# Low halves of gate, branch and output-projection weights made by adding transfers

## The chip, the cores and the metric

The kernel runs on one core of a Trainium2 chip. The core has TensorE (PE in the profile), which multiplies matrices, VectorE (DVE), ScalarE (ACT) and GpSimd (POOL), which work on tiles, and SyncE (SP), which here only issues transfers. Each engine takes its instructions in the order in which they were written for it, and waits at an instruction until the semaphores it needs are set. Sixteen DMA engines do the transfers. Tiles lie in SBUF, 128 partitions wide; TensorE writes into eight PSUM banks of 128 x 512 float32.

The metric is the time of one execution on the device in microseconds. The kernel before takes 1569.97 us (median of three runs, 1569.14 to 1570.35).

## The reference

Two layers of a bidirectional encoder, with 512 tokens of 1024 channels in float32. One layer:

```
h = rms_norm(x);  proj = h @ w_in
c_q, c_kv, k_rope, gq, gk, gv, pool_in, gate_logits = split(proj)
o_mla  = mla_branch(c_q, c_kv, k_rope, ...)    # latent attention, 8 heads
o_gqa  = gqa_branch(gq, gk, gv, ...)           # 8 query heads, 2 key heads
o_pool = pool_branch(pool_in, ...)             # windows 2, 4, 8, 16
gates  = sigmoid(gate_logits)                  # 3 x 1024 per token
merged = gates[0] * (o_mla @ w_branch_mla) + gates[1] * (o_gqa @ w_branch_gqa)
       + gates[2] * (o_pool @ w_branch_pool)
x = x + merged @ w_out
u = depthwise_conv(rms_norm(x) @ ffn_w_up);  u_gate, u_val = split(u)
x = x + (silu(u_gate) * u_val) @ ffn_w_down
```

## The kernel before

**Two halves.** TensorE takes operands in a rounded float32 form (fp32r). To keep float32's accuracy, each operand is written as a rounded high half and the low half that the rounding left, and a product is three matmuls (`mm3`, which calls `mm`, line 522): high x high, high x low, low x high. For a weight the halves are `wh` and `wl`, for the normalised input `HH` and `HL`, for the merged branches `mgh` and `mgl`, for the branch outputs pairs such as `oph` and `opl`, for softmax numerators `ph` and `pl`.

**The stream of weights.** All weights come in one stream, in the order of use. SyncE's queue fetches stretches of up to 1024 columns into `raw` tiles, of which there are three; one holds two pieces of 512 columns. A piece of 512 columns is four 128 x 128 blocks, and for 512 tokens it feeds 4 x 3 matmuls. `_widths` lists the pieces of a layer up to the FFN, `_layer_units` adds those of the FFN and gives each a kind, and `_stream` deals them onto transfers. `w_split` makes the halves of the next piece. For kind "p", ScalarE copies the piece into `wh` (line 296, a helper's line that all of ScalarE's operations have), and VectorE or GpSimd subtracts it from the raw piece into `wl` (line 303, likewise a helper's); `pick` takes the engine by what the planner's clock holds free first, with a bias (`W_BIAS`, 2.54 us). For kind "u", which before only some pieces of the FFN have, `by_transfer` is used, as it also is for three of the seven forms in which the FFN's down weights come (there the tiles are named `fh` and `fl`):

```
A.activation(hi, r, AF.Copy)                      # high half, rounded
A.activation(lo, f(hi), AF.Copy, scale=-1.0)      # its negative
nc.gpsimd.dma_start(f(lo), r, accum_op=ALU.add)   # line 434: raw is added on
```

The transfer is issued from GpSimd's queue and adds the raw piece to the negated high half in SBUF. A raw tile is free for the next fetch when the low half of its last piece is done.

`wnext` hands out the next piece and has the pieces ahead of it split. How far ahead depends on the kinds that come:

```
kinds_ = [units[min(j + i, len(units) - 1)][0] for i in (0, LAP, LAF)]
n = LAF if any(k not in "pu" for k in kinds_) else LAP if "u" in kinds_[:2] else LA
```

with `LA, LAP, LAF = 3, 4, 6`. The pairs `wh`, `wl` have six buffers.

**What sets the order.** A planner in the kernel's Python keeps a clock (`Clock`) with a cost for each operation and a time at which each engine is free. Chains of steps on the other engines are written at the moment at which the clock says that their inputs are ready. So the order in which each engine gets its instructions follows from these costs, and a piece of another kind moves other instructions too: `copy` picks between ScalarE and VectorE by the same clock.

**The stages of a layer.** Input projection, with the pool branch; then the gates and branch products of the three branches (`gates`), 24 gate units of two pieces each and 12 branch units of two pieces. These are used as filler: `attention` goes through a plan of steps for eight heads (score matmuls `ps_S`, whose row maxima `nm` go by a small DMA into a row of the queries, `qb<-nm`; probabilities `ps_ST` or `ps_mi`, exponential on ScalarE, halves `ph` and `pl`; products with the values into `ps_AV`; a running sum `vt`, whose product with `unit` ends a head), and before each step that is not ready by the clock it writes filler units. GQA attention comes first, then the latent (MLA) attention, and what remains of the gates and branches fills in behind. There is one PSUM bank for scores (`S`), and two or one for each of the other tags. While GQA attention runs, the values (`vm`) and queries and keys (`MQ`, `MK`) of the MLA heads are made out of filler. Then comes the output projection, 8 tiles of two pieces each. As each tile ends, VectorE adds it to the residual `XM` and makes the scaled input `hn`, ScalarE the high half `HH` and the squares `sqt`, VectorE `HL`, and GpSimd sums the squares into `sq`; for the FFN's down weights' way of multiplying, sums of tiles (`tt`, `tf`) are made too. The FFN's first up-projection piece follows the output projection without a pause in TensorE's order.

Of the kernel before, what the change touches and what calls it, by code (L numbers as in the profile page):

```python
# [19 lines left out]
T = 512  # L20
D = 1024
KC = D // P
# [52 lines left out]
def _order(br):  # L75

    r, lag = [], LAG[br]
    for m in range(KC + lag):  # L80
        r += [(k, pos.index(m)) for k, b, pos in EXTRA if b == br and m in pos]
        if m < KC:
            r.append(("g", m))
        if m >= lag:
            r.append(("b", m - lag))
    return r


WIDTHS = {"g": [T, T], "b": [T], "q": [384, 384], "n": [256], "v": [256]}
# [3 lines left out]
def _widths():  # L93

    r = [384] * KC + [T] * 8 + [T] * KC + [288] * MID + [T] + [288] * (KC - MID)
    for br in (2, 1, 0):
        late = []
        for k, _ in _order(br):
            if k in "nv":
                late = WIDTHS[k]  # L100
            else:
                r += WIDTHS[k][:1] + late + WIDTHS[k][1:]
                late = []
    return r + [T] * (2 * KC)


def _groups():
# [4 lines left out]
def _ffn():  # L112

    toks, late = [], []
    for g, (c0, c1) in enumerate(_groups()):
        dealt = len(late) - (KEEP * SIZES[g - 1] if g == len(SIZES) - 1 else 0)
        for n, c in enumerate(range(c0, c1)):
            if g == 0:  # L120
                toks += [("u", c, 0), ("u", c, 1)]
                continue
            now = late[:dealt * (n + 1) // (c1 - c0) - dealt * n // (c1 - c0)]
            late = late[len(now):]
            for f in FORMS:
                toks.append(("f", c, f))
                if f in SPOTS:
                    k = SPOTS.index(f)
                    toks += now[len(now) * k // len(SPOTS):len(now) * (k + 1) // len(SPOTS)]
        late += [("d", g, m, i) for m in range(KC) for i in range(c1 - c0)]  # L130
    return toks + late


def _layer_units():

    r = [("p", wd) for wd in _widths()]
    for tok in _ffn():
        if tok[0] == "u":
            r += [("u", T), ("p", T), ("next",)]
        elif tok[0] == "f":  # L140
            r.append(tok)
        elif (tok[2] * SIZES[tok[1]] + tok[3]) % 4 == 0:
            r.append(("u" if tok[1] < len(SIZES) - 1 else "p", T))
    return r


def _stream():
# [4 lines left out]
    for kind, *u in _layer_units() * L:  # L152
        if kind == "next":
            plain = (plain + 1) % (2 * SIZES[0])
            if plain and plain >= 2 * SIZES[0] - 8:
                early.append(len(slots))
                slots.append(T)
                alone.append(True)
            continue
        if kind == "f":  # L160
            if u[1] == FORMS[0]:
                first, fresh = len(pieces), True
                for _ in range(4):
                    if early:
                        pieces.append((early.pop(0), 0, T))
                        continue
                    pieces.append((len(slots), 0, T))
                    slots.append(T)
                    alone.append(True)
            units.append((u[1], first))  # L170
            continue
        if len(slots) <= KC or fresh or alone[-1] or slots[-1] + u[0] > 1024:
            slots.append(0)
            alone.append(False)
        fresh = False
        pieces.append((len(slots) - 1, slots[-1], u[0]))
        slots[-1] += u[0]
        units.append((kind, len(pieces) - 1))
# [1840 lines left out]
```

## Time and profile before

| | |
|---|---|
| median of the runs | 1569.97 us (1569.14 to 1570.35) |
| profiled execution, its own time | 1569.55 us |
| its span in the profile | 1567.7 us |
| TensorE busy | 1546.2 us (99%) |
| VectorE busy | 1171.7 us (75%) |
| ScalarE busy | 1012.9 us (65%) |
| GpSimd busy | 809.8 us (52%) |
| hardware transfer queue q1 | 32.9% of the sixteen DMA engines' span |
| software transfer queue q0 | 19.3% of it |
| granted TensorE clock | 1.00 |

The profile is of one execution. Its span leaves out 1.85 us that lie around it (1569.55 - 1567.7). In rows of instructions stand the line, the engine, the operation, the tile written and those read (buffer numbers left out), the shape, the count, then busy time and mean in ns, then idle time ahead and what ended it. A row of the timeline begins with start and duration in us. Waits are put down to the releaser that came last.

### The profile page before, as it was taken

The numbers are of one execution on the slowest core, as the hardware profiler recorded it, in microseconds if no ns is written. First come the engines' busy times: TensorE is split into PE (matmuls) and PEld (weight loads), VectorE is DVE, ScalarE is ACT, GpSimd is POOL, SyncE is SP. The second block draws the span as 40 slices with busy tenths as digits, with TensorE's granted clock in tenths as the row PEclk, the third lists the DMA queues.
The fourth block names the chain that finished last, engine by engine and source line by source line (L and its number), as shares of the span: only waits on it lengthen the run. The fifth ranks groups of instructions, "written<-read, shape, count | busy, mean of one in ns | idle before, by whom it ended". The sixth has DMA issues, their size and how long they took to land.

```text
span 1567.7 us, 24155 instructions
## 1 busy us (share of the span) xinstructions
PE 1546.2 (99%) x8265; PEld 1339.0 (85%) x8265; DVE 1171.7 (75%) x1932; ACT 1012.9 (65%) x1908; POOL 809.8 (52%) x822
## 2 busy tenths in 40 slices
PE   9999989999999999999999999899999999999999
PEld 8888878888878999999898888788887789999997
DVE  6867886875777888877756688768757778888785
ACT  5557766763457878777544577666635577777763
POOL 3984867764653222222488658768546533222222
PEclk9999999999999999999999999999999999999999
DMA  5432224313378877886434322343243688787863
GB/s 201 126 115 80 75 74 145 118 66 124 108 181 199 194 179 174 193 195 145 130 120 133 114 74 70 93 135 115 59 143 108 176 200 201 166 192 174 211 119 101
DMA packets 124684, 216.61 MB, mean 138 GB/s; under 512 B 29328, under 2 KB 51344, under 8 KB 124560
## 3 DMA queue, kind: packets, MB, share of 16 engines
q1 hardware_dynamic: 91152, 162.93, 32.9%
q0 software_dynamic: 28512, 51.92, 19.3%
q8 instruction: 65, 1.06, 0.3%
q10 hardware_dynamic: 4896, 0.21, 0.2%
q14 instruction: 59, 0.48, 0.1%
HBM read 149.41 MB, written 13.63 MB: 104 GB/s over the span
## 4 chain that ended last, share of the span: by engine, by line
PE 84%; DVE 7%; issue 3%; ACT 3%; POOL 2%; DMA 1%; SPq 0%; ACTq 0%; POOLq 0%; DVEq 0%
PE ps_acc L522 35%; PE ps_AV L522 16%; PE ps_ST L522 14%; PE ps_S L522 10%; PE ps_mi L522 10%; DVE XM L303 1%; DVE tt L303 1%; POOL wl L303 1%; DMA wl<-raw 1%; DVE mgl L303 1%; ACT mgh L296 1%; DVE sq L303 0%; DVE gt L307 0%; ACT wh L296 0%; DVE XM L307 0%
## 5 line engine op out<-in xcount | busy, mean ns | idle before, releaser
L303 POOL TENSOR_TENSOR wl<-raw,wh 128x512 fp32r<-128x512 f32 (+3 forms) x261 | 335.6, 1292 | 273.3 <-ACT wh L296 252.7
L296 ACT ACTIVATE wh<-raw 128x512 fp32r<-128x512 f32 (+2 forms) x453 | 265.4, 605 | 49.9 <-DVE raw L303 10.5
L434 POOL DMA_DIRECT2D wl<-raw x96 | 83.7, 872 | 246.8 <-ACT sx L296 160.4
L434 POOL DMA_DIRECT2D fl<-raw x102 | 89.2, 874 | 154.2 <-ACT fl L296 69.2
L522 PE MATMUL ps_acc<-HH,wl 128*128 128x512 f32 x416 | 163.2, 392 | 4.4 <-DMA wl<-raw 4.4
L522 PE MATMUL ps_acc<-HH,wh 128*128 128x512 f32 x416 | 163.4, 393 | 3.9 <-DVE vm L303 2.9
L522 PE MATMUL ps_acc<-HL,wh 128*128 128x512 f32 x416 | 162.8, 391 | 0.4 <-DVE HL L303 0.4
L307 DVE SCALAR_TENSOR_TENSOR a<-u,prm,a 128x511 f32<-128x511 f32 x176 | 133.7, 761 | 34.9 <-ACT a L296 34.1
L311 DVE TENSOR_REDUCE nm<-ps_S 128x1 fp32r<-128x512 f32 x128 | 87.7, 685 | 36.1 <-PE ps_S L522 34.7
L296 ACT ACTIVATE a<-u,prm 128x512 f32<-128x512 f32 x88 | 71.2, 811 | 63.2 <-DVE u L303 63.2
L522 PE MATMUL ps_acc<-tf,wh 128*128 128x256 f32 x544 | 100.1, 282 | 0.0
L522 PEld LDWEIGHTS ps_acc<-HH,wl 128*128 128x128 f32 x416 | 78.1, 188 | 23.1 <-DMA wl<-raw 6.2
L522 PEld LDWEIGHTS ps_acc<-HH,wh 128*128 128x128 f32 x416 | 78.3, 188 | 20.7 <-issue 4.4
L522 PEld LDWEIGHTS ps_acc<-tf,wh 128*128 128x128 f32 x544 | 88.5, 189 | 6.2
L522 PEld LDWEIGHTS ps_acc<-HL,wh 128*128 128x128 f32 x416 | 78.2, 188 | 17.1 <-DVE HL L303 1.1
L303 DVE TENSOR_TENSOR wl<-raw,wh 128x512 fp32r<-128x512 f32 (+2 forms) x97 | 71.7, 740 | 25.5 <-ACT wh L296 25.3
L522 PE MATMUL ps_AV<-HH,wh 128*128 128x256 f32 (+1 forms) x248 | 82.1, 331 | 0.0
L522 PE MATMUL ps_AV<-HH,wl 128*128 128x256 f32 (+1 forms) x248 | 82.0, 331 | 0.0
L522 PE MATMUL ps_AV<-HL,wh 128*128 128x256 f32 (+1 forms) x248 | 82.0, 331 | 0.0
L522 PE MATMUL ps_acc<-tf,wl 128*128 128x256 f32 x272 | 76.6, 282 | 0.0
L296 ACT ACTIVATE ps_ST<-ps_ST 128x512 f32<-128x512 f32 x86 | 49.8, 581 | 33.1 <-PE ps_ST L522 31.7
L296 ACT ACTIVATE fl<-fh 128x512 fp32r<-128x512 f32 x102 | 64.5, 633 | 3.2
(428 smaller groups left out, 4969.7 us busy)
## 6 DMA issues: line engine op xcount, KB each, us to landing
raw<-w SPq DMA_DIRECT2D x160, 512.0 KB, 3.7
raw<-w SPq DMA_DIRECT2D x140, 256.0 KB, 4.3
fl<-raw POOLq DMA_DIRECT2D x102, 256.0 KB, 5.4
wl<-raw POOLq DMA_DIRECT2D x96, 256.0 KB, 4.6
raw<-w SPq DMA_DIRECT2D x14, 384.0 KB, 3.0
XM<-x SPq DMA_DIRECT2D x16, 256.0 KB, 3.1
dtq<-tr SPq DMA_DIRECT2D x16, 192.0 KB, 1.9
dtk<-tr SPq DMA_DIRECT2D x16, 192.0 KB, 2.0
```

The costliest lines, as they stand in the source:

```text
L296: return self.eng.activation(out, in_, func, **k)
L303: return self.eng.tensor_tensor(out, *a)
L307: return self.eng.scalar_tensor_tensor(out, *a)
L311: return self.eng.tensor_reduce(out, in_, *a, **k)
L434: nc.gpsimd.dma_start(f(lo), r, accum_op=ALU.add)
L522: PE.matmul(o, lhsT=lhsT, rhs=rhs, start=start, stop=stop, skip_group_check=again)
```

## The change

The gate and branch pieces of all three branches and the pieces of the output projection get the kind "u"; for that `_widths` returns pairs of kind and width. These are 48 + 24 + 16 = 88 pieces in each layer. The input projection, the latent attention's own weights (kinds q, n, v of the order) and the FFN keep what they had.

```
 def _widths():
 
     r = [384] * KC + [T] * 8 + [T] * KC + [288] * MID + [T] + [288] * (KC - MID)
+    r = [("p", wd) for wd in r]
     for br in (2, 1, 0):
         late = []
         for k, _ in _order(br):
+            ws = [("u" if k in "gb" else "p", wd) for wd in WIDTHS[k]]
             if k in "nv":
-                late = WIDTHS[k]
+                late = ws
             else:
-                r += WIDTHS[k][:1] + late + WIDTHS[k][1:]
+                r += ws[:1] + late + ws[1:]
                 late = []
-    return r + [T] * (2 * KC)
+    return r + [("u", T)] * (2 * KC)
...
 def _layer_units():
 
-    r = [("p", wd) for wd in _widths()]
+    r = _widths()
```

Since `wnext` looks ahead by `LAP` where such pieces come, their halves are asked for four pieces ahead where it was three. The order of the engines moves as follows; the lines of the changed kernel are two further down.

TensorE at the end of layer 0's GQA attention. Before, the last piece of filler (`wh69`, `wl69`, out of which rows of the gate are left for later) stands ahead of the last head's probabilities:

```order
L522 MATMUL ps_acc_364_2375<-HH_81,wh69_2312 128x512
L522 MATMUL ps_acc_364_2375<-HL_82,wh69_2312 128x512
L522 MATMUL ps_acc_364_2375<-HH_81,wl69_2313 128x512
L522 MATMUL ps_ST_386_2479<-qa_323_2107,ka_80_594 128x512
L522 MATMUL ps_ST_386_2479<-qb_324_2108,kb_81_595 128x512
L522 MATMUL ps_AV_378_2433<-ph_376_2431,vg_76_590 128x512
```

After, the same piece stands ahead of the head before, and the four score matmuls of the last head (`ps_S`) come behind it:

```order
L524 MATMUL ps_acc_344_2339<-HL_82,wh69_2263 128x512
L524 MATMUL ps_acc_344_2339<-HH_81,wl69_2264 128x512
L524 MATMUL ps_ST_363_2446<-qa_324_2207,ka_80_594 128x512
L524 MATMUL ps_ST_363_2446<-qb_325_2208,kb_81_595 128x512
L524 MATMUL ps_S_367_2452<-ka_80_594,qa_326_2209 128x512
L524 MATMUL ps_AV_354_2386<-ph_352_2384,vg_76_590 128x512
L524 MATMUL ps_AV_354_2386<-pl_334_2253,vg_74_588 128x512
L524 MATMUL ps_S_368_2462<-ka_80_594,qa_326_2209 128x512
```

The next filler follows 24 attention matmuls later before, 45 after; in both, it starts at row 1010 of TensorE's order.

GpSimd at the end of the output projection in layer 0 (`wl129` is the first piece of the FFN). Before:

```order
L303 TENSOR_TENSOR wl127_4537<-raw67_4422,wh127_4536 128x512
L303 TENSOR_TENSOR sq_711_4267<-sq_711_4267,sqt_730_4498 128x512
L303 TENSOR_TENSOR wl128_4561<-raw67_4422,wh128_4560 128x512
L434 DMA wl129_4565<-raw68_4485 128x512
L303 TENSOR_TENSOR sq_711_4267<-sq_711_4267,sqt_740_4558 128x512
```

After:

```order
L436 DMA wl127_4591<-raw67_4530 128x512
L436 DMA wl128_4624<-raw67_4530 128x512
L305 TENSOR_TENSOR sq_711_4347<-sq_711_4347,sqt_730_4588 128x512
L436 DMA wl129_4652<-raw68_4581 128x512
L305 TENSOR_TENSOR wl130_4678<-raw68_4581,wh130_4677 128x512
```

The subtractions of `wl127` and `wl128` have become issues of transfers, and the sum of squares stands right ahead of `wl129`'s transfer.

GpSimd at the first gate pieces of layer 0 (`raw_863` holds the first two). Before:

```order
L303 TENSOR_TENSOR gqr_804<-gqr_804,rp_115_909 128x512
L303 TENSOR_TENSOR wl_963<-raw_863,wh_962 128x512
L303 TENSOR_TENSOR yt_806<-y_102_805,ssr_347 128x32
L303 TENSOR_TENSOR yt_806<-yt_806,y_102_805 128x32
L315 TENSOR_SCALAR yt_806<-yt_806 128x32
L303 TENSOR_TENSOR y_102_805<-yt_806,y_102_805 128x32
L303 TENSOR_TENSOR wl_988<-raw_863,wh_987 128x512
```

After:

```order
L436 DMA wl_930<-raw_863 128x512
L305 TENSOR_TENSOR gqr_804<-gqr_804,rp_115_909 128x512
L436 DMA wl_967<-raw_863 128x512
L305 TENSOR_TENSOR yt_806<-y_102_805,ssr_347 128x32
L305 TENSOR_TENSOR yt_806<-yt_806,y_102_805 128x32
```

The first transfer stands ahead of the rotary sum `gqr`, the second ahead of the small steps (`yt`, `y`) that make a reciprocal root, where before the subtractions came behind each.

Counted over the program, GpSimd's order has 176 transfers more and 166 subtractions fewer, VectorE's 10 subtractions fewer and some copies out of PSUM more (`MK` 0 to 6, `MQ` 2 to 10, `vm` 6 to 12, `ph` 46 to 52), and ScalarE's 176 negated copies more and those other copies fewer. TensorE has the same matmuls.

## The prediction

> **What bounds the kernel now.** I read the page first (busy times, costliest groups, DMA issues), then TensorE's waits, then windows of 20 us, then the timeline where a window falls short.
>
> ```profile
> span 1567.7 us, 24155 instructions
> PE 1546.2 (99%) x8265; PEld 1339.0 (85%) x8265; DVE 1171.7 (75%) x1932; ACT 1012.9 (65%) x1908; POOL 809.8 (52%) x822
> ```
>
> TensorE (PE) is the bound: 1546.2 of 1567.7 us, so that all its idle time is 21.5 us. The change leaves every matmul as it is; it can win only out of these 21.5 us, and lose by adding to them. The rate that a filled stage keeps:
>
> ```profile
> 351.65 18.38 PE ps_acc L522 x81
> ```
>
> 18.38/81 = 0.227 us for a matmul of 512 columns. Where the idle time lies:
>
> ```profile
> PE ps_acc L522 <- DMA wl<-raw: 4.4, 4, 2.3
> PE ps_acc L522 <- DVE vm L303: 2.9, 2, 1.4
> PE ps_ST L522 <- ACT vt L296: 2.5, 2, 1.3
> PE ps_AV L522 <- DVE ph L319: 1.7, 2, 0.9
> ```
>
> (Columns: tile waited in, releaser, us in all, times, longest.) There are two kinds. The first row is the entry into the FFN, where TensorE meets the first low half made by an adding transfer. The other three come twice each, once in a layer: the end of grouped-query (GQA) attention, where no gate or branch matmuls are left to fill in. Windows of the two places, with one filled stage between (span, then busy time and count of PE, PEld, DVE, ACT, POOL, clock, DMA share, GB/s):
>
> ```profile
> 140.00:160.00 20.00, 20.00 (x96) 16.93 (x95) 16.91 (x32) 16.88 (x32) 8.90 (x18) 1.00 0.25 73
> 200.00:220.00 20.00, 17.29 (x79) 13.90 (x78) 16.44 (x32) 14.03 (x29) 15.41 (x19) 1.00 0.23 79
> 980.00:1000.00 20.00, 16.60 (x72) 12.85 (x70) 17.66 (x33) 14.51 (x29) 14.52 (x18) 1.00 0.19 60
> 420.00:440.00 20.00, 18.59 (x81) 14.75 (x79) 17.73 (x25) 11.78 (x24) 14.14 (x12) 1.00 0.53 145
> 1200.00:1220.00 20.00, 17.48 (x75) 13.63 (x74) 17.62 (x26) 13.20 (x27) 12.79 (x11) 1.00 0.65 172
> ```
>
> **The change part by part.** In both layers 48 gate, 24 branch and 16 output-projection pieces, 176 in all, get their low half by copy, negated copy and adding transfer. The order of the changed kernel has 166 subtractions fewer on GpSimd (POOL), 10 fewer on VectorE (DVE), 176 negated copies more on ScalarE (ACT) and 176 transfers more in POOL's queue. The prices:
>
> ```profile
> L303 POOL TENSOR_TENSOR wl<-raw,wh 128x512 fp32r<-128x512 f32 x227 | 302.1, 1337 | 247.3 <-ACT wh L296 232.3 <-PE ps_acc L522 7.9 <-issue 2.9
> L303 DVE TENSOR_TENSOR wl<-raw,wh 128x512 fp32r<-128x512 f32 x83 | 61.5, 741 | 19.3 <-ACT wh L296 19.2
> L296 ACT ACTIVATE wl<-wh 128x512 fp32r<-128x512 f32 x96 | 60.7, 633 | 3.0
> L434 POOL DMA_DIRECT2D wl<-raw x96 | 83.7, 872 | 246.8 <-ACT sx L296 160.4
> wl<-raw POOLq DMA_DIRECT2D x96, 256.0 KB, 4.6
> q0 software_dynamic: 28512, 51.92, 19.3%
> ```
>
> Engine time: POOL 176 x 0.872 - 166 x 1.337 = -68 us; DVE -10 x 0.741 = -7 us, less some 20 copies out of PSUM that come over from ACT; ACT 176 x 0.633 = +111 us, less those copies. None of it is on PE's path by itself. The software queue took 19.3% of the span for 51.92 MB, 198 transfers of 256 KB, that is 0.193 x 1567.7/198 = 1.53 us of all sixteen engines each; 176 more are +269 us, some 17 points of share. In the gate stages (0.25) that is covered.
>
> Latency of one low half from the end of its high half: before 1.34 us; after 0.63 + 4.6 = 5.2 us, so 3.9 us later. The lookahead grows from 3 to 4 pieces where these pieces come, and one piece of four token blocks by three terms is 12 matmuls, 12 x 0.227 = 2.7 us. So a low half comes 1.2 us nearer to its use in a stage of PE work alone, and less where attention matmuls stand between. The slack in most of the attention stage is several us, which covers this. It is thin at the first gates:
>
> ```profile
> 97.12 1.48 POOL L303 TENSOR_TENSOR wl<-raw,wh 128x512 fp32r<-128x512 f32 x1
> 99.28 0.40 PE L522 MATMUL ps_acc<-HH,wl 128*128 128x512 f32 x1
> ```
>
> Made at 98.60, used at 99.28: slack 0.7 us, 1.2 later makes 0.5 us of stall, in each layer: **+1.0** (0 if the earlier high half is early enough; up to 3 if POOL, whose queue also holds the pool branch's and norm's work here, issues late).
>
> **Entry of the FFN.** Timeline of layer 0, and the releaser in layer 1:
>
> ```profile
> 422.36 0.48 DVE L315 TENSOR_SCALAR hn<-XM,prm 128x512 f32<-128x512 f32 x1
> 425.87 1.50 POOL L303 TENSOR_TENSOR sq<-sq,sqt 128x512 f32<-128x512 f32 x1
> 426.24 0.63 ACT L296 ACTIVATE wl<-wh 128x512 fp32r<-128x512 f32 x1
> 427.32 1.48 POOL L303 TENSOR_TENSOR wl<-raw,wh 128x512 fp32r<-128x512 f32 x1
> 427.57 1.51 DVE L315 TENSOR_SCALAR hn<-XM,prm 128x512 f32<-128x512 f32 x1
> 428.75 1.05 POOL L434 DMA_DIRECT2D wl<-raw  x1
> 434.98 0.50 PE L522 MATMUL ps_acc<-HH,wl 128*128 128x512 f32 x1 [1.00 <-DMA wl<-raw]
> ```
>
> ```profile
> 1206.59 0.92 POOL L434 DMA_DIRECT2D wl<-raw  x1
> 1214.13 0.50 PE L522 MATMUL ps_acc<-HH,wl 128*128 128x512 f32 x1 [2.29 <-DMA wl<-raw]
> ```
>
> The negated copy of the first FFN piece was done at 426.87, but its transfer was issued only at 428.75, behind the norm's sum and the last subtraction. Without that subtraction it goes at about 427.4, 1.3 us sooner; the wait of 1.00 goes, and of 2.29 about 1.3. The same row shows the other gain: the tensor_scalar that makes hn took 1.51 us beside POOL's subtraction, and 0.48 five microseconds earlier, and the reason that I see is POOL's subtraction of two SBUF inputs; so VectorE's chain to the next HH should quicken too. I take 1.0 + 1.3 + 0.2 = **-2.5**. The ends: -6, if all losses of both windows (1.4 + 2.5 us of PE's 20 in each) go and some 2 more at the later FFN pieces and the merge; +1, if the transfers now crowd one another. For that end, the landing times of this stage, from 425 to 480 us and from 1198 to 1212 us:
>
> ```profile
> DMA to landing us min/median/max: 3.3/5.9/6.8
> ```
>
> ```profile
> DMA to landing us min/median/max: 4.4/6.0/7.5
> ```
>
> In the output projection a piece is wanted every 2.7 us, and its transfer takes 1.53 us of the DMA engines: 0.56 of share on the raw loads. If that pushes landings past 7.5 us, the gain of layer 1 is lost.
>
> **End of GQA attention.** Here the change moves instructions. Before, 24 attention matmuls stand behind the last gate fill (215.31 to 224.55 us); after, 45, the scores of the last head among them.
>
> ```profile
> 202.88 0.40 PE L522 MATMUL ps_S<-ka,qa 128*128 128x512 f32 x1
> 203.38 1.58 DVE L303 TENSOR_TENSOR wl<-raw,wh 128x512 fp32r<-128x512 f32 x1
> 206.56 0.47 PE L522 MATMUL ps_acc<-HH,wh 128*128 128x512 f32 x1 [1.44 <-DVE vm L303]
> 211.71 0.68 DVE L311 TENSOR_REDUCE nm<-ps_S 128x1 fp32r<-128x512 f32 x1
> 212.46 0.48 ACTq L1385 DMA_DIRECT2D qb<-nm  x1
> 215.31 0.39 PE L522 MATMUL ps_ST<-qa,ka 128*128 128x512 f32 x1
> 224.55 0.39 PE L522 MATMUL ps_acc<-HH,wh 128*128 128x512 f32 x1
> ```
>
> ```profile
> qb<-nm ACTq DMA_DIRECT2D x16, 2.0 KB, 1.9
> ```
>
> ```profile
> L303 DVE TENSOR_TENSOR pl<-ps_ST,ph 128x512 fp32r<-128x512 f32 x86 | 58.5, 683 | 10.4 <-ACT ph L296 9.3
> ```
>
> Before, the last head's first score matmul ran at 202.88 and attention ended at 224.55: 21.67 us for 70 matmuls' worth of work (73, six of half width), 15.9 us, so 5.8 us lost. After, I lay the chain out by hand. The four score matmuls stand within ten rows and share one PSUM bank, so each waits for the row maximum of the one ahead: 0.39 + 0.68 and an estimated 0.2 of handoffs is 1.27 us, four times 5.1, and a pl of 0.68 stands in VectorE's order ahead of the last maximum: 5.8 us. The maxima then go by DMA, 1.9 us to landing, with another 0.3 of handoffs until the head's first probability matmul: 8.0 us for 19 matmuls, 4.3 us of work. Then come the same 24 matmuls as before, 9.24 us for 5.5 of work. Lost: 3.7 + 3.8 = 7.5 us, and VectorE comes about 1 us later to that point than before (eleven of its steps, some 0.7 us each, stand from the first maximum to where it was at 215.31 before: 7.7 us without any idle of its own), so 8.5 against 5.8: **+2.7 in each layer, +5.4**. Ends: 0, if the wait for vm of 1.44 goes with the subtraction at 203.38 and VectorE, which POOL delays less, has the scores ready sooner; +4.5 in each layer, +9, if ScalarE, 16.88 of 20 us busy at 140 us and given three or four copies more of 0.63 there, falls a further head behind.
>
> **The sum.** +5.4 + 1.0 - 2.5 = +3.9 on the profiled execution, 1569.55 us with 1.85 around the span; the runs' median is 1569.97. On that: 1573.9. What a measurement can tell from no change is about 0.2%, 3.1 us.
>
> **A rule against it.** The Trainium skill, "SBUF — State Buffer", section on the two separate sides, says that a transfer issued from GpSimd's queue cannot have its descriptors written while VectorE holds the shared port pair in a 2-port mode, and advises hardware queues. Here the issue beside hn took 1.05 us against a mean of 0.872, so the trace agrees in direction, with 0.2 us. By the rule each transfer would wait up to one such step of VectorE (0.48 us), and the sum would rise by at most that at the two thin places, some 1 us in all. My sum leaves it out.
>
> **The rivals.**
> 1. *The FFN entry wins more than the tail loses* (other side: faster). Mechanism: POOL's subtractions no longer stretch VectorE's two-input steps, in the output projection and at the end of GQA attention. For it: 1.51 against 0.48 above, and 1.58 for a DVE subtraction whose mean is 0.741. Against it: at the tail nearly all DVE steps read PSUM and take their 0.68 regardless. It decides where the tail costs under 1 us in each layer: -6 + 1 + 1 = -4, 1566.
> 2. *Terms cancel.* The tail at +1.3 in each layer (the wait for vm goes), first gates +0.5, entry -3.5: -0.4, 1569.6.
> 3. *Transfers land late.* If the share at 420 us (0.53) and 0.56 more saturate the DMA engines, raw tiles are held until the transfer is done, loads start later, and PE waits for wl through the output projection: 1 us for perhaps four of sixteen pieces, in each layer, on top of the sum without its gain: +6.4 + 8 = +14, 1584. Against it: one piece's 0.5 MB half-load and transfer fit 2.7 us, by 1.53 and the load's part.
> 4. *The order does not matter*, as the fill that is spent early is work that VectorE uses to catch up: part of 2.
>
> **Numbers.** Forecast (1572.5 to 1581): 0.46. Rival 1: 0.29. Rival 2 with 4: 0.20. Rival 3: 0.05. Slower by over 0.2% takes most of the forecast and rival 3 (0.49), within 0.2% the rest of the forecast and nearly all of rival 2 (0.22), faster rival 1 (0.29). The likeliest is 1573.9; its own range is 1572 to 1580. The range that leaves out no more than 2 in 10 goes from 1563.5 (near rival 1's full -6 with no tail loss) to 1581.
>
> **What would show it.** Tail: waits of PE in a window of some 25 us up to the end of GQA attention, now for DVE nm or a row DMA, 8 us and more; right if the layer loses 2 us or more there over before, wrong if under 1. First gates: a PE wait for DMA wl<-raw near 85 to 100 us. Entry: the wait for wl at 434 us gone, that at 1214 halved, hn at 0.5 to 0.6 us. ACT +111 us busy at most, POOL about 740, DMA share of the software queue near 36%. The forecast falls if the tail's loss stays at 5.8 us, or if PE waits for wl all along the output projection.

## The result and the profile after

The changed kernel takes 1577.41 us (median of four, 1575.26 to 1578.93) against 1569.56 (median of four): 1.005 times the time before, 95% interval 1.0037 to 1.0063. It is slower, as forecast; the forecast was 1573.9. The profiled execution took 1575.26 us with a span of 1573.4, 5.7 more than before.

The page of the changed kernel: span, busy times, the software queue and the groups that grew.

```profile
span 1573.4 us, 24580 instructions
PE 1550.5 (99%) x8265; PEld 1340.9 (85%) x8265; DVE 1146.9 (73%) x1940; ACT 1113.5 (71%) x2066; POOL 744.3 (47%) x832
q0 software_dynamic: 53856, 98.07, 36.3%
L436 POOL DMA_DIRECT2D wl<-raw x272 | 244.7, 907 | 508.6 <-ACT wl L298 235.5
L298 ACT ACTIVATE wl<-wh 128x512 fp32r<-128x512 f32 x272 | 172.0, 633 | 8.6
...
wl<-raw POOLq DMA_DIRECT2D x272, 256.0 KB, 4.5
```

The work moved as counted: POOL fell by 65.5 us to 744.3, ACT rose by 100.6, the software queue's share went from 19.3% to 36.3%. TensorE did the same matmuls and was busy 4.3 us longer, of which the clock, below, has a part. What TensorE waits for has turned round:

```profile
PE ps_S L524 <- DVE nm L313: 5.2, 10, 1.0
PE ps_ST L524 <- DMA qb<-nm: 3.1, 4, 1.2
PE ps_acc L524 <- DVE MQ L321: 2.0, 2, 1.0
PE ps_acc L524 <- DVE XM L309: 1.7, 2, 1.0
PE ps_ST L524 <- DVE vt L309: 1.5, 2, 0.7
```

The wait for low halves at the FFN's entry, 4.4 us, is gone from the list. In its place stand waits for row maxima and for their small transfers, and two for copies of MLA queries out of PSUM (`MQ`), which before were ScalarE's. Windows of 20 us over the places of the prediction, in its columns:

```profile
80.00:100.00 20.00, 19.09 (x96) 15.89 (x95) 12.33 (x23) 14.59 (x33) 18.54 (x29) 1.00 0.85 191
100.00:120.00 20.00, 19.01 (x87) 15.68 (x86) 10.69 (x22) 11.62 (x21) 6.62 (x9) 1.00 0.81 178
220.00:240.00 20.00, 18.02 (x70) 12.98 (x70) 16.23 (x32) 16.83 (x33) 7.65 (x10) 0.91 0.32 70
420.00:440.00 20.00, 20.00 (x90) 16.56 (x89) 15.84 (x25) 13.46 (x27) 9.60 (x10) 1.00 0.87 223
1200.00:1220.00 20.00, 20.00 (x90) 16.58 (x89) 16.37 (x26) 12.36 (x25) 9.95 (x10) 1.00 0.93 240
```

The end of the output projection is now full, 20.00 of 20 in both layers where it was 18.59 and 17.48, though the DMA share there is 0.87 and 0.93. (The same point of the program comes 4.0 and 6.6 us later now; windows moved by that, 424 to 444 and 1206.6 to 1226.6 us, have TensorE at 20.00 and 19.67.) The first gates, 20.00 in both windows before, are not. The end of GQA attention lies some 7 us later than before and shows fewer matmuls, and a mean clock of 0.91. Its timeline in layer 0, with the head before last's row of maxima ahead:

```profile
208.54 0.48 ACTq L1387 DMA_DIRECT2D qb<-nm  x1
213.90 0.51 PE L524 MATMUL ps_ST<-qb,kb 65*128 65x512 f32 x1 [1.23 <-DMA qb<-nm]
214.25 0.40 PE L524 MATMUL ps_S<-ka,qa 128*128 128x512 f32 x1
215.43 0.62 PE L524 MATMUL ps_S<-ka,qa 128*128 128x512 f32 x1 [0.32 <-DVE nm L313]
217.04 0.62 PE L524 MATMUL ps_S<-ka,qa 128*128 128x512 f32 x1 [0.53 <-DVE nm L313]
218.44 0.62 PE L524 MATMUL ps_S<-ka,qa 128*128 128x512 f32 x1 [0.32 <-DVE nm L313]
219.82 0.48 ACTq L1387 DMA_DIRECT2D qb<-nm  x1
221.73 0.50 PE L524 MATMUL ps_ST<-qb,kb 65*128 65x512 f32 x1 [0.34 <-DMA qb<-nm]
...
228.55 0.63 PE L524 MATMUL ps_AV<-ph,vg 128*128 128x512 f32 x1
228.97 0.63 PE L524 MATMUL ps_AV<-pl,vg 128*128 128x512 f32 x1
231.44 0.39 PE L524 MATMUL ps_acc<-HH,wh 128*128 128x512 f32 x1
```

The four scores start 1.40 us apart on average ((218.44 - 214.25)/3), the row leaves 5.57 us after the first score, and attention ends 17.2 us after it. That is the chain of the prediction. New are the transfer issued at 208.54, which landed only at some 213.8 (its counterpart in layer 1 also took 5.3 us), and, in this layer alone, matmuls at the very end that start 0.42 us apart.

To compare kernels I add up what each matmul starts later than TensorE's rate allows after the one ahead, stage by stage, from the starts in the trace (losses under 0.08 us left out). Both layers together, in us; "gates" reaches from the end of the input projection to the third head of attention, "attention" from there through GQA and MLA attention, "entry" over merge, output projection and the FFN's first pieces.

| kernel | gates | attention | entry | span |
|---|---|---|---|---|
| before | 1.0 | 13.9 | 9.4 | 1567.7 |
| changed | 6.1 | 23.9 | 1.8 | 1573.4 |

So the change lost 5.1 + 10.0 us and won 7.6. That is 7.5 in these stages, while the span rose by 5.7; outside them the same count has about 1 us less than before (4.9 and 3.8), and what falls under 0.08 us is not counted. Of the 10.0, the ends of GQA attention have 3.5 and 3.3 (5.4 to 8.9 and 5.5 to 8.7), and the rest lies earlier in attention.

### The profile page after: what moved, and what is told of

It is laid out like the page before. It is cut to its first block, busy times and chain, and to the rows that moved or that the text cites. A ratio compares the mean times of both kernels' runs of the same rounds, so it can differ in the third digit from the quotient of the medians.

```text
span 1573.4 us, 24580 instructions
## 1 busy us (share of the span) xinstructions
PE 1550.5 (99%) x8265; PEld 1340.9 (85%) x8265; DVE 1146.9 (73%) x1940; ACT 1113.5 (71%) x2066; POOL 744.3 (47%) x832
## 3 DMA queue, kind: packets, MB, share of 16 engines
q0 software_dynamic: 53856, 98.07, 36.3%
## 5 line engine op out<-in xcount | busy, mean ns | idle before, releaser
L436 POOL DMA_DIRECT2D wl<-raw x272 | 244.7, 907 | 508.6 <-ACT wl L298 235.5
L298 ACT ACTIVATE wl<-wh 128x512 fp32r<-128x512 f32 x272 | 172.0, 633 | 8.6
L305 POOL TENSOR_TENSOR wl<-raw,wh 128x512 fp32r<-128x512 f32 (+3 forms) x95 | 116.9, 1239 | 94.3 <-ACT wh L298 92.1
L524 PEld LDWEIGHTS ps_acc<-HH,wl 128*128 128x128 f32 x416 | 78.1, 188 | 16.9
L305 DVE TENSOR_TENSOR wl<-raw,wh 128x512 fp32r<-128x512 f32 (+2 forms) x87 | 60.7, 698 | 22.4 <-ACT wh L298 22.2
L305 DVE TENSOR_TENSOR pl<-ps_ST,ph 128x512 fp32r<-128x512 f32 x86 | 58.8, 684 | 19.5 <-ACT ph L298 19.1
```

The costliest lines, as they stand in the source:

```text
L298: return self.eng.activation(out, in_, func, **k)
L305: return self.eng.tensor_tensor(out, *a)
L524: PE.matmul(o, lhsT=lhsT, rhs=rhs, start=start, stop=stop, skip_group_check=again)
```

## The experiments

**One part alone.** First the output projection's transfers without the gates' and branches', then the other way round. The edits against the changed kernel:

```
# e1_out_only
-            ws = [("u" if k in "gb" else "p", wd) for wd in WIDTHS[k]]
+            ws = [("p", wd) for wd in WIDTHS[k]]
# e2_gates_branches
-    return r + [("u", T)] * (2 * KC)
+    return r + [("p", T)] * (2 * KC)
```

> Only the output projection's pieces are made by adding transfers; gates and branches keep the subtraction, and TensorE's order around grouped-query attention is that of before. Theory (the gain at the entry of the FFN is the output projection's own, the losses are the gates'): idle time at the merge, the entry and the first FFN pieces falls from 9.5 us (4.2 and 5.3 in the two layers) to about 2, the attention tails stay at 5.4 each: some 1562. Rival (the entry gains only because the gates' work is off GpSimd too): 1568 to 1570.

> Only gate and branch pieces are made by adding transfers; the output projection keeps the subtraction. Theory: tails 8.8 us in each layer instead of 5.4, the stretch from the first gates to the third head some 3.5 us more in each, the entry as before: 1569.6 + 6.7 + 7 = 1583. Rival (the losses come from the output projection's transfers holding the raw tiles): 1570.

The first took 1563.58 us, 0.9958 of before (0.9945 to 0.9970); its losses were 0.9, 14.0 and 2.6. The second took 1582.55, 1.008 (1.0066 to 1.0094), with 6.6, 23.8 and 8.8. Both theories held, to 2 us. The gain is the output projection's own, and all the loss is that of the gates and branches. In the first, the tails are those of before, by the same three waits, and no low half is waited for:

```profile
PE ps_acc L524 <- DVE vm L305: 2.9, 2, 1.5
PE ps_ST L524 <- ACT vt L298: 2.5, 2, 1.3
PE ps_AV L524 <- DVE ph L321: 1.7, 2, 0.9
```

**The order alone.** The changed kernel's order to the last row, with a subtraction in the place of each copy and transfer:

```
     def by_subtraction(hi, lo, r):
         A.activation(hi, r, AF.Copy)
+        A._count(lo, 0.00084, 0.18)        # the planner counts the copy that isn't made
         ck.free["Pool"] = max(ck.free.get("Pool", 0.0), ck.fin + ck.SEM)
         ck.took("Pool", D_ISSUE)
-        nc.gpsimd.dma_start(f(lo), r, accum_op=ALU.add)
+        nc.gpsimd.tensor_tensor(lo, r, f(hi), ALU.subtract)
         ck.fin += D_ADD
```

> The changed kernel's order of instructions on every engine to the last row, its lookahead of four and its planner's costs, but all 176 pieces get their low half by subtraction on GpSimd: no negated copy, no transfer. Theory (the tail is lost by the order alone): the tail loses 8 to 9 us in each layer as in the changed kernel, the entry loses what it lost before: about 1569.6 + 6.7 = 1576, and up to 3 more where the score matmuls wait early in attention. Rival (the tail is lost by the negated copies on ScalarE and by the later low halves): the tail loses about 5.5, 1570.

It took 1574.82 us, 1.0033 (1.0022 to 1.0044), with losses of 4.6, 21.3 and 4.0; its tails lost 8.3 and 9.2. TensorE waits for the same maxima and sums as in the changed kernel:

```profile
PE ps_S L535 <- DVE nm L313: 5.7, 10, 1.5
PE ps_S L540 <- DVE gk L305: 2.0, 2, 1.6
PE ps_ST L535 <- DVE vt L309: 1.5, 2, 0.7
PE ps_ST L535 <- ACT vt L298: 1.5, 2, 0.7
```

So 11.0 of the 15.1 us that the changed kernel loses up to the end of attention are lost by its order even with the old work in it. Its entry, 4.0 with every subtraction in place, also shows that less than I thought of the gain there is the transfers'.

**Another order for the same work.** If the order costs so much, an order with the fill at its old place should win it back. Two ways: the planner's `SLACK`, how far fill may run ahead, at 20 instead of 35; and a planner that is not told of the gates' copies and transfers.

```
# e6_slack20
-SLACK = 35
+SLACK = 20
# e9_planner_unseen, for gates and branches
+        nc.scalar.activation(lo, f(hi), AF.Copy, scale=-1.0)      # not counted
+        G._two(lo)                                                # a subtraction is counted
         nc.gpsimd.dma_start(f(lo), r, accum_op=ALU.add)
```

> The changed kernel with the planner's SLACK at 20 instead of 35 (in the kernel before, that number changes no row of the order on any engine): now 24 attention matmuls stand behind the last gate fill again, the last head's scores ahead of it. Theory (order): the tail is back at about 5.4 us in each layer, 6.7 less than the changed kernel, the rest unchanged: about 1569 to 1570. Rival (ScalarE's load or the transfers are behind the tail): the wait moves but stays, 1575 to 1577.

> All 176 pieces by adding transfers as in the changed kernel, but for gates and branches the planner is not told: it charges no negated copy, it charges GpSimd a subtraction instead of the issue, adds no time for the transfer, and keeps the lookahead of three; so 24 attention matmuls stand behind the last gate fill, as before. Theory (the losses come from the order that the planner writes): tails 5.4 us each, first gates and early attention up to 1 us more than before in each layer, entry 0.9 each: 1562 to 1564. Rival (176 real negated copies and 3.9 us more of latency cost the time): tails 8 us or more, waits for wl and for probabilities in attention, 1573 to 1580.

As times, both expectations of the theory failed, though the tails themselves came back. The first took 1578.94 us, 1.005 (1.0036 to 1.0064), losses 7.8, 26.7 and 2.5. (Its executions took 1575.79 to 1581.08, and the profile is of the slowest; 1.6 of the 7.8 are a stretch at half clock.) Its tails lost 4.0 us in each layer, where the changed kernel's lost 8.9 and 8.7, so the tail does follow the order. But its longest waits in attention are now scores that wait for POOL's low half of the queries, all four ahead of the tails:

```profile
PE ps_S L524 <- POOL qa L305: 7.1, 4, 2.4
PE ps_S L524 <- DVE nm L313: 2.8, 4, 1.0
```

The second took 1582.62 us, 1.008 (1.0065 to 1.0095), losses 4.3, 32.8 and 1.2. Its tails together lose less than before (9.2 against 10.9), but MLA attention, which lost 0.2 before, now loses 12.7 us in both layers, and GQA attention 20.1. The longest waits are for two transfers of row maxima:

```profile
PE ps_mi L534 <- DMA qa<-nm: 4.7, 2, 2.6
```

So the order is not the cause by itself: there is a load for which the planner makes room. Where it does, the losses up to the end of attention are 15.1 us above those of before; where it doesn't, 22.2. This second run also keeps the lookahead of three pieces, and 2.5 us of its waits are for low halves made by transfers, so that not all of the 22.2 is the load's.

**Which load.** Two kernels with the order of before to the last row put one half of that load on top of the old subtractions, uncounted by the planner: the copies alone, and transfers of the same size alone.

```
# e13_copies_alone, ahead of each gate and branch subtraction
+            nc.scalar.activation(lo[:, :wd], f(hi[:, :wd]), AF.Copy, scale=-1.0)
# e14_transfers_alone, behind it
+            nc.gpsimd.dma_start(slot("idle")[:, :wd], r)
```

> The kernel before with its order to the last row; only, each gate and branch piece's negated copy is written by ScalarE too, ahead of the subtraction that then overwrites it (144 copies of 0.63 us, no transfer, the planner not told). The changed kernel in an order like before's lost 37 us in gates, attention and merge of both layers, against 15 before. Theory A (ScalarE's copies cost it): a good part of these 22 us here, 1577 or more. Theory B (the low halves' later arrival costs it): the copies find room, some 0.63 us less slack, 1570 to 1573.

> The kernel before with its order on every engine; only, behind each gate and branch piece's subtraction GpSimd issues a transfer of the raw piece, 256 KB, into a tile that nobody reads (144 transfers, written plainly, not added; no negated copy; the planner not told). With the copies alone, which cost 25 us, this splits the changed kernel's load into its two parts. In the changed kernel the small transfers of the row maxima took 2.9 us in the median instead of 1.9, and 5.3 at worst. Theory (the traffic slows these small transfers, which attention waits for, but it is the smaller part): the row maxima take 2.5 us or more, 1573 to 1578. Rival (only ScalarE's copies matter): 1569.5 to 1571.

The copies alone took 1594.88 us, 1.016 (1.0146 to 1.0173): 25 us for 144 copies that nobody reads, with no transfer. Losses 2.6, 33.1 and 14.1; ScalarE was busy 1100.3 us, against 1113.5 in the changed kernel.

```profile
PE 1558.7 (98%) x8265; PEld 1341.2 (84%) x8265; DVE 1178.3 (74%) x1932; ACT 1100.3 (69%) x2052; POOL 809.7 (51%) x822
```

```profile
PE ps_S L526 <- DVE nm L313: 6.3, 10, 1.1
PE ps_acc L526 <- DVE gt L309: 4.2, 6, 0.9
PE ps_acc L526 <- DMA wl<-raw: 3.5, 4, 1.9
PE ps_ST L526 <- ACT vt L298: 3.1, 2, 1.6
```

Theory A holds in so far as copies without any transfer are enough for the loss, and in attention TensorE waits for no low half. At the last branch products of each layer its weight loads waited 1.1 and 1.3 us for ScalarE itself. But the run adds more than a load on ScalarE: the copy writes the tile that the subtraction then overwrites, so the subtraction waits for it. In the changed kernel no step of VectorE stands between a gate's copy and its low half. Here VectorE was held up by the copies in eight places, and it waited longer for probabilities too (16.9 us before):

```profile
DVE wl L305 <- ACT wl L461: 15.1, 8, 2.8
DVE pl L305 <- ACT ph L298: 23.7, 38, 1.4
```

At 69% of the span ScalarE is far from busy all the time; but it works in order, and its steps (exponential, halves, gates) stand in chains with VectorE and TensorE. My reading is that inside attention such a chain has no 0.63 us to spare. How much of the 25 us is that, and how much is VectorE waiting behind the copies, this run does not separate.

The transfers alone took 1604.43 us, 1.0219 (1.0195 to 1.0244), losses 5.4, 42.4 and 10.7. This one tells little. It also gave POOL 82 us more of issues beside all its subtractions, and took buffers and raw tiles until each transfer landed, for which VectorE and SyncE then waited:

```profile
L462 POOL DMA_DIRECT2D idle<-raw x144 | 82.2, 571 | 0.8 <-PE ps_ST L526 0.7
L305 DVE TENSOR_TENSOR pl<-ps_ST,ph 128x512 fp32r<-128x512 f32 x86 | 58.6, 683 | 16.5 <-ACT ph L298 9.9 <-DMA idle<-raw 2.2 <-PE ps_AV L526 1.9
SPq L405 <- DMA idle<-raw: 420.5, 72, 11.5
```

Its theory is not borne out in its numbers either: in layer 0 the transfers of the maxima kept a median of 1.9 us, at worst 3.9 (2.7 before); those of GQA attention in both layers (`qb<-nm`) went to 2.3, between the 1.9 of before and the 2.9 of the changed kernel. What transfers cost attention by themselves stays open.

**Why the entry won 7.6.** The kernel before with the longer lookahead in the output projection alone; and the output projection's transfers with POOL kept at its old subtractions beside them, for the first 14 pieces of each layer:

```
# e7_lookahead_out, against the kernel before: pieces marked "x" are subtracted like "p"
-        n = ... else LAP if "u" in kinds_[:2] else LA
+        n = ... else LAP if "u" in kinds_[:2] or "x" in kinds_[:2] else LA
# e11_pool_beside, against e1_out_only
+                nc.gpsimd.tensor_tensor(slot("idle")[:, :wd], r, f(hi[:, :wd]), ALU.subtract)
```

> The kernel before, with one thing changed: in the output projection the halves are asked for four pieces ahead instead of three; all low halves are still subtracted. The run of the order alone lost only 2.0 us at the entry of the FFN in each layer, with subtractions. Theory A (the longer lookahead brought that): the entry's loss falls from 9.4 us in both layers to about 4, 1565. Theory B (it needs the transfers, since the subtraction of the last piece stands ahead of the first FFN transfer): it stays at 9, 1569 to 1570.

> The kernel with transfers in the output projection only, and behind each of its first 14 transfers in each layer GpSimd also does a subtraction of the old form and size into a tile that nobody reads; the order is otherwise the same on every engine. Theory (GpSimd's subtractions stretch VectorE's two-input steps, and with it the entry): hn and the sums of tiles take up to 1.5 us again and the entry loses 2 to 4 us more, 1565 to 1567. Rival (the transfers help only by going earlier): VectorE's steps get longer but the entry keeps its 2.5 us, 1563.6.

The first took 1568.22 us, 0.9988 (0.9979 to 0.9998), and lost 7.5 at the entry. Neither theory had it right: the wait for the FFN's first low half is gone, as A said, but a wait for HH stands there instead, of which the kernel before had 0.6 us:

```profile
PE ps_acc L524 <- ACT HH L298: 3.5, 2, 1.8
```

So the low half and the input's high half had both come late, and both had to come sooner. The second took 1589.87 us, 1.0124 (1.0109 to 1.0139), and lost 30.1 at the entry: far more than either theory had. The tensor_scalar that makes hn, from 400 to 440 us, before, in e1_out_only and here:

```profile
L315 DVE TENSOR_SCALAR hn<-XM,prm 128x512 f32<-128x512 f32 x7 | 5.7, 811 | 0.1
```

```profile
L317 DVE TENSOR_SCALAR hn<-XM,prm 128x512 f32<-128x512 f32 x7 | 4.6, 656 | 0.2
```

```profile
L317 DVE TENSOR_SCALAR hn<-XM,prm 128x512 f32<-128x512 f32 x6 | 10.6, 1759 | 0.4
```

The mean goes from 811 to 656 ns without POOL's subtractions, and to 1759 with them beside the transfers. POOL's subtraction itself took 1.60 us there and up to 2.24, against 1.337 on average. So the two engines do hold each other up, and taking the subtractions away wins by that as well as by the earlier transfers; since here the dummies also delay the transfers queued behind them, how much is whose is not separated.

**Fewer pieces.** Transfers for the output projection and the MLA branch's gates and products (used in and behind MLA attention); and for the output projection and all branch products.

```
# e12_out_and_mla
+            ws = [("u" if k in "gb" and br == 0 else "p", wd) for wd in WIDTHS[k]]
# e16_out_and_branches
+            ws = [("u" if k in "b" else "p", wd) for wd in WIDTHS[k]]
```

> Transfers for the output projection and for the gates and branch of the MLA branch alone (that is 24 gate and branch pieces of 72 in each layer, used behind and within MLA attention, where ScalarE is 8 to 14 of 20 us busy); GQA's filler keeps the subtraction. Theory: the GQA tail stays at 5.4 us, the merge loses nothing more, 1562 to 1564 like the output projection alone; rival: MLA attention, without losses before, now loses 3 us or more, 1567 up.

> Transfers for the output projection and all branch products, gates keep the subtraction (24 + 16 pieces in each layer). Theory (the cost goes with the pieces that ScalarE must copy inside GQA attention, a third of the changed kernel's here): tails and attention lose 2 to 5 us more than with the output projection alone, 1566 to 1569. Rival: no cost below some number of pieces, 1563.6.

The first took 1562.41 us, 0.9953 (0.9939 to 0.9967), not told apart from e1_out_only by its interval. Its time is the theory's, but its profile, of the slowest of five executions (1566.90), shows what the rival said: MLA attention lost 6.3 us, where with the output projection alone it lost 0.2. Of this, 2.9 are lost at two waits for row maxima, one of whose transfers took 7.1 us to land, and 2.5 by matmuls at half clock:

```profile
PE ps_ST L524 <- DMA qa<-nm: 2.3, 2, 1.9
```

The second took 1570.85, 1.0006 (0.9997 to 1.0015), losses 4.3, 18.1 and 1.8, above what its theory said: 24 pieces in each layer, 16 of them for the two branches whose products fill GQA and early MLA attention, already use up the whole gain of the output projection. Both kernels have 40 transferred pieces in each layer and differ by 8.4 us, so their number alone does not decide; where they are used, and the order that the planner writes for that, does.

## Why the prediction was right, and where its sizes were wrong

The direction and the mechanism at the end of GQA attention came out as laid out by hand; the sizes of two other terms did not, and one loss was not in the sum at all. That the time still fell within the range is partly luck: the entry won 5.1 us more than forecast, while the first gates lost 4.1 more and attention ahead of its last heads 3.2 that I had put at nothing.

**End of GQA attention: +2.7 in each layer.** Measured +3.5 and +3.3. The chain from the last head's first score on was right step by step (5.57 us to the row's departure against 5.8; 17.2 us in all against 8.0 + 9.24). The 1 us of lag that I added for VectorE does not show in it. What the working did not have stands ahead of it: the head before waits for a row of maxima whose transfer took 5.3 us, which loses 1.5 us in each layer. The half clock in layer 0 cost nothing here: in layer 1, at full clock, the same stretch took 17.2 us too.

**First gates: +0.5 in each layer.** Measured +2.6 on average. The wait for a low half that I priced is there, at 83.58 us, with 0.22 us. The larger waits are for VectorE: `MQ` (2.0 us) and `XM` (1.7). The planner had taken copies off ScalarE, now busier, and put them into VectorE's queue, where they stand behind other steps and, as I read it, free a PSUM bank later. I had listed these copies, and costed them at nothing.

**"None of it is on PE's path by itself."** This step failed. I costed ScalarE's 111 us at nothing because its share was 65%, and used it only as a bound for the tail. In the order of before, the copies alone, with the subtractions waiting behind them, cost 25 us (e13_copies_alone), and the copies with their transfers lose 22.2 us up to the end of attention with a planner that is not told (e9_planner_unseen). The order that the planner writes around them brings that to 15.1, but this order loses 11.0 even with the old work in it (e5_order_alone). So the copies were not free; how the loss divides between ScalarE's load, the transfers and the order stays open. The 16.88 of 20 us in the window at 140 us, which I quoted, was the row to go by.

**Entry: -2.5.** Measured -7.6 (4.1 to 0.8 and 5.3 to 1.0). The end that I gave for it was -6. I had priced the earlier transfer, and only 0.2 beside it; the waits of the merge (0.8 and 0.9 before), for HH and of the later FFN pieces went too. That VectorE was held up by POOL's subtractions is part of the reason (e11_pool_beside). The order and the longer lookahead are another part, since e5_order_alone lost only 4.0 there with every subtraction in place. My fear that transfers would crowd one another at 0.56 of share each did not come true: the share reached 0.93 with no wait for a low half there.

**The rule against it.** The trace does not bear out the Trainium skill's warning ("SBUF — State Buffer", the two separate sides) at a size that counts here: the mean issue went from 872 to 907 ns, and the transfers' median landing from 4.6 to 4.5 us.

**Rivals.** The faster one came true in its mechanism (entry -7.6) but not in its condition, since the tails cost 3.4 each and not under 1; it is the kernel e1_out_only. The one in which the terms cancel had the tail at +1.3, and it was +3.4. The one with transfers landing late at the output projection is refuted: no wait for a low half is left there.

The sum by terms was +3.9; the span rose by 5.7, and the median by 7.9. The median is higher because the profiled execution was the fastest of the four. Why the others took some 2 to 4 us more stays open; their mean clocks were 0.996, 0.999 and 0.997 against its 0.999.

## What to carry to other kernels

An engine that is 65% busy over the span may have no free time in a stage where its steps stand in a chain with the bounding engine: look at the stage's window, and at each step's place in the queue, before a copy is costed at nothing. Where a planner writes the order, price the work that it moves as carefully as the work that is added: here the new order alone, with copies on another engine and filler spent earlier, lost 11.0 us. Move work off a contended engine where the engine that takes it over has room (here the output projection, 0.9958), and leave it where it has none.

## What the runs showed of the hardware beyond that

**The clock can fall after a thinly filled stretch.** In the changed kernel TensorE's clock halved for some 3.4 us at the end of layer 0's attention, in the windows

```profile
224.00:228.00 4.00, 2.52 (x9) 1.75 (x9) 3.45 (x8) 3.88 (x9) 2.71 (x3) 0.92 0.00 0
228.00:232.00 4.00, 4.00 (x12) 2.65 (x12) 3.99 (x7) 2.38 (x5) 1.28 (x1) 0.65 0.00 0
...
1004.00:1008.00 4.00, 2.38 (x8) 1.23 (x8) 3.50 (x8) 3.88 (x9) 2.96 (x4) 1.00 0.00 0
```

and eight matmuls started 0.43 us apart instead of 0.227; layer 1's stretch, just as thin (2.38 of 4 us), kept 1.00. Here the half clock cost nothing: VectorE's last running sum, for which the end of attention waits, starts 16.05 us after the last head's first score in layer 0 (at 214.25) and 16.04 in layer 1 (at 995.26).

```profile
230.30 0.74 DVE L309 SCALAR_TENSOR_TENSOR vt<-ps_ST,vg,vt 128x512 fp32r<-128x512 f32 x1
1011.30 0.74 DVE L309 SCALAR_TENSOR_TENSOR vt<-ps_ST,vg,vt 128x512 fp32r<-128x512 f32 x1
```

Where it meets filler, it does cost. In e12_out_and_mla it came right behind layer 1's tail and lost 1.6 us:

```profile
1002.00:1005.40 3.40, 3.40 (x9) 2.64 (x8) 2.03 (x5) 2.05 (x4) 1.28 (x1) 0.50 0.39 138
```

So idle time at the bound can cost more than itself, if the thin stretch is what brings the half clock on; these runs show only that it comes behind some such stretches and not behind others. It does not explain how much executions of one kernel differ: e16_out_and_branches had spans of 1570.9 us at a mean clock of 1.0 and 1566.8 at 0.999. The Trainium skill, "TensorE: Matmul & The Clock Gate", Part 1, tells of such halving by windows of about 3.4 us of activity that run free of the program. The length and the rate agree; but TensorE was busy for 63% of the four microseconds ahead, not idle.

**Small transfers became slower beside large ones.** The 2 KB rows of maxima of GQA attention in both layers, 1.9 us in the median before, in the changed kernel:

```profile
qb<-nm ACTq DMA_DIRECT2D x16, 2.0 KB, 2.9
```

All rows of layer 0's attention, GQA and MLA, in the changed kernel (1.9, 1.9 and 2.7 before):

```profile
DMA to landing us min/median/max: 1.9/2.2/5.3
```

The worst took 5.3 us, and TensorE waited 3.1 us for four of them, in both layers. The `qb` rows had 2.9 with transfers for gates and branches alone too (e2_gates_branches), and 1.9 with the output projection's alone (e1_out_only). With plain transfers of the same size in the gates and branches (e14_transfers_alone) they had 2.3. The adding transfers hold the DMA engines longer: 144 plain ones raised the software queue's share from 19.3% of 1567.7 us to 25.1% of 1601.3, some 0.7 us each of all sixteen engines, against 1.5 for an adding one. Whether that is why was not tried.
